# First FFN projections feature block by feature block over three weight tiles; the joins' lo parts and sums of squares on VectorE

## The chip, the cores and the metric

The kernel runs on one core of a Trainium2 chip. The metric is the device time of one execution in microseconds. All products run on TensorE (PE), which accumulates in PSUM banks. VectorE (DVE), ScalarE (ACT) and GpSimd (POOL) work between them, and SyncE (SP) issues the transfers. Each engine takes its instructions strictly in the order in which they stand in its own queue; semaphores make one wait for another.

## The reference

The reference is a two-layer backbone over 512 latent tokens and 256 context tokens of width 1024, in fp32:

```python
h = modulate(rmsnorm(x), m[0], m[1])
y = even_mixer(h_ctx, h_lat, ...) if i % 2 == 0 else odd_mixer(h_ctx, h_lat, ...)
x = x + m[2] * y
x = x + m[5] * conv_ffn(modulate(rmsnorm(x), m[3], m[4]), ffn_w_up[i], ffn_conv_w[i], ffn_conv_b[i], ffn_w_down[i])

def conv_ffn(h, w_up, conv_w, conv_b, w_down):
    u = h @ w_up                                  # 1024 -> 2 x 2816
    u = conv(u, width 3 over tokens) + conv_b
    a, gate = split(u, 2)
    return (a * silu(gate)) @ w_down
```

The even mixer (layer 0) is differential attention beside pooling, the odd one (layer 1) a gated linear recurrence in both directions. Both end in an output projection. In layer 1 the context is not carried on after the mixer. At the end stands `rmsnorm(x) * final_norm`.

## The kernel before

The streams lie with features on the partitions: eight feature blocks of 128 (`KT`), f = 0 to 7, tokens along the free axis. `xl` holds the latents, `xc` the context. An fp32 product is made of three matmuls with rounded parts: a value is split into a hi part, its rounding (ACT, L153 or L541), and a lo part, the rest (DVE, L154 or L542). `up` (L167) then adds, for each feature block, wh x hh, wh x hl and wl x hh into one PSUM bank; every matmul goes through the helper at L137. A weight tile is 128 x 1024 values: its wh comes from L153, its wl from L154.

A **join** is the stretch in which one stage's output projection ends and the next stage's first projection begins. There are four: A (even out-projection into FFN 0), B (last down-projection of FFN 0 into the odd mixer), C (odd out-projection into FFN 1) and D (last down-projection of FFN 1 into the final norm). At a join tokens go by 256: A and B have three such segments, two of latents and the context, C and D two. For each segment and each f, the following happens:

- PE makes the product into a bank, and `residual` (L198, DVE) adds it into the stream. Its read frees the bank.
- `acc_add` (L493 to L506) squares the new stream on ACT (L502 for f below 2, L505 for the others) and adds the square into one of two sums, `acc`, by L506. For f = 3, 4, 5 the sum runs on GpSimd, for 2, 6, 7 on DVE. The squares lie in two buffers.
- When all f are done, `norm` (L525) multiplies the sums by a matrix of ones on PE and takes rstd on ACT (L350, L352). Then, for each f, it scales (L540, DVE), makes hh (L541, ACT) and hl (L542, DVE).

The norm of a segment runs between the next segment's products. The last segment's is left over as an iterator, `self.todo`, which the next stage takes up: at A the norm of the context, at C that of the second half of the latents.

The FFN goes over 22 pairs of weight tiles. Its first pair is special. `ffn_pre` (L545) makes three of its four weight tiles ahead of time, during the out-projection; in layer 1 the lo parts of the second and third are made on GpSimd. `first_gated` (L609) then multiplies: for each segment, each block of 256 tokens and each of the three tiles, all eight f, so 24 matmuls in a row on one bank. The rest of `todo` is taken up after the third tile of the first block in layer 0, after the first tile in layer 1. The fourth tile is split after that (its buffers are those of the first tile) and multiplied over all tokens. `conv` and `gate` (L646, L654) follow on ACT and DVE. The banks of the FFN turn over seven PSUM tiles.

The Tile framework orders each engine's instructions from the program text and its own rules; the fences in the section on the change show what came of it.

Of the kernel before, what the change touches and what calls it, by code (L numbers as in the profile page):

```python
# [16 lines left out]
ALU = mybir.AluOpType  # L17
# [3 lines left out]
P = 128  # L21
D = 1024
KT = D // P
NL = 512
NC = 256
# [90 lines left out]
class Net:  # L116
# [376 lines left out]
    def acc_add(self, f, seg):  # L493
        nc = self.nc
        o, n = seg
        i = f % 2
        if f == 0:
            self.acc[o] = self.t(self.np, [P, 2, NC], "acc")
        acc = self.acc[o][:, i, :]
        x = self.xres(f, seg)  # L500
        if f < 2:
            nc.scalar.activation(acc, x, AF.Square)  # L502
            return
        sq = self.t(self.np, [P, NC], "sq2")
        nc.scalar.activation(sq, x, AF.Square)  # L505
        (nc.gpsimd if f in (3, 4, 5) else nc.vector).tensor_tensor(acc, acc, sq, op=ALU.add)  # L506

    def segmented(self, segs, body, then, first=3, rate=1, defer=False):
        todo = iter(())
# [35 lines left out]
    def ffn_pre(self, l):  # L545
        nc, Wu = self.nc, self.a["ffn_w_up"][l]
        ra, rg = self.load_cols(Wu, 0), self.load_cols(Wu, DFF)
        ws = []
        self.pre = (ra, rg, ws)
        for raw, j in ((ra, 0), (rg, 0), (ra, 1)):  # L550
            eng = nc.gpsimd if l and ws else nc.vector
            ws.append(self.split(raw[:, :, j * P:(j + 1) * P], eng=eng))
            yield

    def odd_pre(self):
# [53 lines left out]
    def first_gated(self, l, segs):  # L609
        nt = segs[-1][0] + segs[-1][1]  # L610
        ra, rg, ws = self.pre
        ws = list(zip((0, FT, 1), ws))
        cs = {i: self.t(self.tmp, [P, nt], "cv", bufs=4) for i, _ in ws}
        for seg in segs:
            o, n = seg
            outs = [self.t(self.ps, [P, NL], "mm", bufs=self.mmbufs)[:, :n] for _ in ws]
            for p in range(0, n, NC):
                for (i, w), out in zip(ws, outs):
                    self.up(w, out[:, p:p + NC], (o + p, NC))
                    if l or i == 1:  # L620
                        for _ in self.todo:
                            pass
            for (i, _), out in zip(ws, outs):
                self.conv(l, i, cs[i], out, seg)
        gs = [self.gate(cs[0], cs[FT])]
        i, w = FT + 1, self.split(rg[:, :, P:2 * P])
        cs[i] = self.t(self.tmp, [P, nt], "cv", bufs=4)
        for seg in segs:
            out = self.t(self.ps, [P, NL], "mm", bufs=self.mmbufs)[:, :seg[1]]
            self.up(w, out, seg)  # L630
            self.conv(l, i, cs[i], out, seg)
        return gs + [self.gate(cs[1], cs[i])]
# [779 lines left out]
```

## Time and profile before

| | us |
|---|---|
| median of three runs | 1778.73 |
| the runs | 1779.82, 1777.18, 1778.73 |
| profiled execution | 1778.03 |
| its span | 1776.2 |
| PE busy | 1730.6 (97%) |
| DVE busy | 1146.7 (65%) |
| ACT busy | 711.5 (40%) |
| POOL busy | 75.5 (4%) |

The mean granted clock of TensorE is 0.992 of full speed (2.4 GHz); at 0.50 it runs at 1.2 GHz. In a timeline row the first number is the start in us from the span's start, the second the duration, and what stands in brackets is the idle time of that engine just ahead, with the releaser that the profile infers. A duration contains a latency, so on a full engine the starts lie closer than the durations say.

### The profile page before, as it was taken

To read this page: it belongs to the slowest core of one execution; us is meant where nothing else is said; L and a number is where in the kernel's file an instruction comes from. 1 tells how busy PE (TensorE), PEld (TensorE's weight loads), DVE (VectorE), ACT (ScalarE), POOL (GpSimd) and SP (SyncE) were. 2 spreads that over 40 slices of the span, in tenths; PEclk is the share of its full clock that TensorE was granted. 3 is DMA by queue.
4 is the path that set the end of the run, shared out by engine and by line. 5 is a ranking of instruction groups with operands and counts; after the bars stand their busy time and mean duration, and the time that the engine had idled before them with its cause. 6 is when DMAs were issued, how large, how long until landed. Compare 5 with 4: busy or idle time off the path is not lost.

```text
span 1776.2 us, 29058 instructions
## 1 busy us (share of the span) xinstructions
PE 1730.6 (97%) x12223; PEld 1471.9 (83%) x12223; DVE 1146.7 (65%) x2109; ACT 711.5 (40%) x1310; POOL 75.5 (4%) x80
## 2 busy tenths in 40 slices
PE   7899989999999999999999999999999999999998
PEld 4687878888888888888889888888878888888887
DVE  5534786785556555656568356666798866656657
ACT  4435564453223232222345424444454533333334
POOL 0202210010000000000001000000000200000001
PEclk9999989999999999999999999999999999999999
DMA  9233113334323432323130211111212132232231
GB/s 319 87 98 97 47 46 104 113 119 167 119 96 116 146 119 96 119 95 119 48 119 1 89 58 49 49 49 49 73 49 95 49 99 91 95 113 86 87 118 48
DMA packets 115478, 165.78 MB, mean 93 GB/s; under 512 B 3211, under 2 KB 98579, under 8 KB 115347
## 3 DMA queue, kind: packets, MB, share of 16 engines
q1 hardware_dynamic: 115043, 163.76, 27.4%
q8 instruction: 96, 1.57, 0.4%
q14 instruction: 35, 0.29, 0.0%
q10 hardware_dynamic: 304, 0.16, 0.0%
HBM read 161.82 MB, written 2.10 MB: 92 GB/s over the span
## 4 chain that ended last, share of the span: by engine, by line
PE 90%; DVE 5%; ACT 2%; DMA 1%; issue 1%; POOL 0%; SPq 0%; DVEq 0%; ACTq 0%; POOLq 0%
PE mm L137 78%; PE sc L137 3%; PE o L137 2%; PE pm L137 2%; PE lv L137 2%; PE tr L137 1%; DVE sq L540 1%; PE tp L1328 1%; DVE hl L542 1%; DMA mraw<-in_w_mod_dram 1%; PE tr L1032 0%; DMA raw<-in_ev_w_in_dram 0%; DVE xl L198 0%; DVE wl L154 0%; ACT wh L153 0%
## 5 line engine op out<-in xcount | busy, mean ns | idle before, releaser
L137 PE MATMUL mm<-hh,wh 128*128 128x512 f32 (+1 forms) x1800 | 636.3, 354 | 5.6 <-ACT hh L541 3.9
L137 PE MATMUL mm<-hh,wl 128*128 128x512 f32 (+1 forms) x1800 | 625.2, 348 | 0.0
L137 PE MATMUL mm<-hl,wh 128*128 128x512 f32 (+1 forms) x1800 | 623.9, 347 | 0.0
L137 PEld LDWEIGHTS mm<-hh,wh 128*128 128x128 f32 x1800 | 339.1, 189 | 57.1 <-issue 10.7
L137 PEld LDWEIGHTS mm<-hh,wl 128*128 128x128 f32 x1800 | 339.2, 188 | 44.4
L137 PEld LDWEIGHTS mm<-hl,wh 128*128 128x128 f32 x1800 | 339.4, 189 | 42.5
L154 DVE TENSOR_TENSOR wl<-raw,wh 128x1024 fp32r<-128x1024 f32 x193 | 234.7, 1225 | 215.3 <-ACT wh L153 211.7
L153 ACT ACTIVATE wh<-raw 128x1024 fp32r<-128x1024 f32 x195 | 203.9, 1057 | 387.7 <-PE mm L137 369.9
L650 DVE SCALAR_TENSOR_TENSOR cv<-mm,colC,cv 128x511 f32<-128x511 f32 (+1 forms) x264 | 173.3, 658 | 112.5 <-ACT cv L648 108.9
L198 DVE SCALAR_TENSOR_TENSOR xl<-mm,mod,xl 128x512 f32<-128x512 f32 (+1 forms) x252 | 170.8, 687 | 45.1 <-PE mm L137 44.8
L137 PE MATMUL mm<-gh,wh 128*128 128x512 f32 (+1 forms) x448 | 159.6, 356 | 0.0
L137 PE MATMUL mm<-gh,wl 128*128 128x512 f32 (+1 forms) x448 | 159.5, 356 | 0.0
L137 PE MATMUL mm<-gl,wh 128*128 128x512 f32 (+1 forms) x448 | 159.3, 356 | 0.0
L648 ACT ACTIVATE cv<-mm,colC 128x512 f32<-128x512 f32 (+1 forms) x132 | 91.6, 695 | 144.2 <-PE mm L137 144.2
L137 PEld LDWEIGHTS mm<-gh,wl 128*128 128x128 f32 x448 | 84.1, 188 | 13.1
L137 PEld LDWEIGHTS mm<-gl,wh 128*128 128x128 f32 x448 | 84.1, 188 | 13.0
L137 PEld LDWEIGHTS mm<-gh,wh 128*128 128x128 f32 x448 | 84.1, 188 | 12.8
L137 PE MATMUL mm<-wh,hh 128*128 128x256 f32 x288 | 82.3, 286 | 2.0 <-DVE xc L198 1.2
L137 PE MATMUL mm<-wl,hh 128*128 128x256 f32 x288 | 80.4, 279 | 0.0
L137 PE MATMUL mm<-wh,hl 128*128 128x256 f32 x288 | 80.3, 279 | 0.0
L655 ACT ACTIVATE cv<-cv 128x768 f32<-128x768 f32 (+1 forms) x44 | 32.5, 739 | 92.0 <-DVE cv L650 92.0
L506 POOL TENSOR_TENSOR acc<-acc,sq 128x256 f32<-128x256 f32 x30 | 23.5, 786 | 1047.2 <-ACT sq L505 1046.8
(271 smaller groups left out, 2195.2 us busy)
## 6 DMA issues: line engine op xcount, KB each, us to landing
raw<-in_ffn_w_up_dram SPq DMA_DIRECT2D x44, 1024.0 KB, 5.1
mraw<-in_w_mod_dram SPq DMA_DIRECT2D x14, 2048.0 KB, 7.9
raw<-in_ffn_w_down_dram SPq DMA_DIRECT2D x22, 1024.0 KB, 4.8
raw<-in_hg_w_in_dram SPq DMA_DIRECT2D x20, 1024.0 KB, 5.0
raw<-in_w_mod_dram SPq DMA_DIRECT2D x12, 1024.0 KB
raw<-in_ev_w_in_dram SPq DMA_DIRECT2D x8, 1024.0 KB, 5.3
mraw<-in_w_mod_dram SPq DMA_DIRECT2D x16, 512.0 KB, 10.0
raw<-in_ev_w_out_dram SPq DMA_DIRECT2D x4, 1024.0 KB, 4.9
```

The lines of the kernel that those rows point to most:

```text
L137: self.nc.tensor.matmul(out, lhsT=lhsT, rhs=rhs, start=start, stop=stop)
L153: insts = (self.nc.scalar.activation(hi, view, AF.Copy), (eng or self.nc.vector).tensor_tensor(lo, view, hi.bitcast(F32), op=ALU.subtract))
L154: (eng or self.nc.vector).tensor_tensor(lo, view, hi.bitcast(F32), op=ALU.subtract))
L198: self.nc.vector.scalar_tensor_tensor(x, in0=out, scalar=gate[:, f, cond:cond + 1], in1=x, op0=ALU.mult, op1=ALU.add)
L506: (nc.gpsimd if f in (3, 4, 5) else nc.vector).tensor_tensor(acc, acc, sq, op=ALU.add)
L540: nc.vector.scalar_tensor_tensor(xn, in0=x, scalar=sc, in1=r, op0=ALU.mult, op1=ALU.mult)
L542: nc.vector.scalar_tensor_tensor(hl, in0=xn, scalar=sh, in1=hh.bitcast(F32), op0=ALU.add, op1=ALU.subtract)
L648: self.nc.scalar.activation(c[:, o:o + n], out, AF.Identity, scale=self.conv_col(l, 1, i), bias=self.conv_col(l, 3, i))
L650: self.nc.vector.scalar_tensor_tensor(c[:, o + d:o + n - s], in0=out[:, s:n - d], scalar=self.conv_col(l, tap, i), in1=c[:, o + d:o + n - ...
L655: self.last_silu = self.nc.scalar.activation(cg, cg, AF.Silu)
L1328: self.nc.tensor.transpose(tp[:, c:c + P], in_=p[:, half * 384 + c:half * 384 + c + P], identity=self.ident)
```

## The change

Three edits. First, L506 runs on DVE for every f: 30 sums move from GpSimd, nine at A, nine at B, six at C and six at D. Second, in layer 1 `ffn_pre` makes the lo parts of the second and third tile on DVE. Third, `first_gated` goes over f in the outer loop and over the three tiles in the inner: nine matmuls for each f, three on each bank. The rest of `todo` is taken up after f = 2, that is after 27 matmuls.

```diff
         sq = self.t(self.np, [P, NC], "sq2")
         nc.scalar.activation(sq, x, AF.Square)
-        (nc.gpsimd if f in (3, 4, 5) else nc.vector).tensor_tensor(acc, acc, sq, op=ALU.add)
+        nc.vector.tensor_tensor(acc, acc, sq, op=ALU.add)
...
         for raw, j in ((ra, 0), (rg, 0), (ra, 1)):
-            eng = nc.gpsimd if l and ws else nc.vector
-            ws.append(self.split(raw[:, :, j * P:(j + 1) * P], eng=eng))
+            ws.append(self.split(raw[:, :, j * P:(j + 1) * P]))
             yield
...
             for p in range(0, n, NC):
-                for (i, w), out in zip(ws, outs):
-                    self.up(w, out[:, p:p + NC], (o + p, NC))
-                    if l or i == 1:
+                for f in range(KT):
+                    for (i, w), out in zip(ws, outs):
+                        self.up(w, out[:, p:p + NC], (o + p, NC), (f,))
+                    if f == 2:
                         for _ in self.todo:
                             pass
```

What this makes of PE's queue at join A. `mm_669`, `mm_670` and `mm_671` are the banks of the first, second and third weight tile; the first `mm_671` waits for the residual that empties the last bank of the out-projection, `mm_659`. Before, `mm_669` has 24 matmuls and then `mm_670` 24; this is where `mm_671` begins:

```order
L137 MATMUL mm_670_3815<-hh_8_91,wl_603_3481 128x256
L137 MATMUL mm_670_3815<-hh_8_91,wh_602_3480 128x256
L137 MATMUL mm_670_3815<-hl_9_92,wh_602_3480 128x256
L137 MATMUL mm_670_3815<-hh_8_91,wl_603_3481 128x256
L137 MATMUL mm_671_3816<-hh_8_91,wh_610_3517 128x256
L137 MATMUL mm_671_3816<-hl_9_92,wh_610_3517 128x256
```

Now, from the end of the out-projection on:

```order
L137 MATMUL mm_659_3767<-hh_8_91,q_594_3450 128x256
L137 MATMUL mm_669_3814<-hh_8_91,wh_597_3457 128x256
L137 MATMUL mm_669_3814<-hl_9_92,wh_597_3457 128x256
L137 MATMUL mm_669_3814<-hh_8_91,wl_598_3458 128x256
L137 MATMUL mm_670_3815<-hh_8_91,wh_602_3480 128x256
L137 MATMUL mm_670_3815<-hl_9_92,wh_602_3480 128x256
L137 MATMUL mm_670_3815<-hh_8_91,wl_603_3481 128x256
L137 MATMUL mm_671_3816<-hh_8_91,wh_610_3517 128x256
```

The third tile's first matmul was the 49th of the FFN and is now the seventh.

DVE's queue at join C, up to the last residual, that of `mm_1894`, for which the first matmul of FFN 1 waits. `wl_1874` is the third tile's lo part, `acc` the sum of squares. Before:

```order
L540 SCALAR_TENSOR_TENSOR sq_1887_13704<-xl_6_89,mod14_1079_7385,acc_1855_13554 128x256
L198 SCALAR_TENSOR_TENSOR xl_6_89<-mm_1888_13708,mod12_926_6101,xl_6_89 128x256
L540 SCALAR_TENSOR_TENSOR sq_1890_13719<-xl_6_89,mod14_1079_7385,acc_1855_13554 128x256
L542 SCALAR_TENSOR_TENSOR hl_9_92<-sq_1887_13704,mod13_1014_6814,hh_8_91 128x256
L198 SCALAR_TENSOR_TENSOR xl_6_89<-mm_1891_13723,mod12_926_6101,xl_6_89 128x256
L540 SCALAR_TENSOR_TENSOR sq_1893_13734<-xl_6_89,mod14_1079_7385,acc_1855_13554 128x256
L198 SCALAR_TENSOR_TENSOR xl_6_89<-mm_1894_13738,mod12_926_6101,xl_6_89 128x256
```

And now:

```order
L506 TENSOR_TENSOR acc_1878_13655<-acc_1878_13655,sq2_1889_13716 128x256
L540 SCALAR_TENSOR_TENSOR sq_1890_13719<-xl_6_89,mod14_1079_7385,acc_1855_13554 128x256
L198 SCALAR_TENSOR_TENSOR xl_6_89<-mm_1891_13723,mod12_926_6101,xl_6_89 128x256
L154 TENSOR_TENSOR wl_1874_13633<-raw_1856_13556,wh_1873_13632 128x1024
L542 SCALAR_TENSOR_TENSOR hl_9_92<-sq_1890_13719,mod13_1014_6814,hh_8_91 128x256
L506 TENSOR_TENSOR acc_1878_13655<-acc_1878_13655,sq2_1892_13731 128x256
L540 SCALAR_TENSOR_TENSOR sq_1893_13734<-xl_6_89,mod14_1079_7385,acc_1855_13554 128x256
L198 SCALAR_TENSOR_TENSOR xl_6_89<-mm_1894_13738,mod12_926_6101,xl_6_89 128x256
```

Sums that GpSimd made, and the third tile's lo part, stand ahead of the last residual. From the residual of `mm_1860` on (the first of three in the row at 1382.08 below) up to that of `mm_1894`, the queue held 14 residuals, 4 sums, 3 of L540 and 1 of L542; now it holds 14, 11 sums, 2 lo parts of weights, 3 and 2. The same count at A, from the residual at 353.65 to that of `mm_659`, differs by nine sums alone.

PE's queue at join C, where the fourth tile (`wh_1918`) begins. Its split waits until the first tile, `wh_1858`, is no longer read. Before, the last matmul that reads `wh_1858` stands 38 places ahead of this:

```order
L137 MATMUL mm_1906_13783<-hh_8_91,wh_1873_13632 128x256
L137 MATMUL mm_1906_13783<-hl_9_92,wh_1873_13632 128x256
L137 MATMUL mm_1906_13783<-hh_8_91,wl_1874_13633 128x256
L137 MATMUL mm_1921_13985<-hh_8_91,wh_1918_13980 128x512
L137 MATMUL mm_1921_13985<-hl_9_92,wh_1918_13980 128x512
L137 MATMUL mm_1921_13985<-hh_8_91,wl_1919_13981 128x512
```

And now:

```order
L137 MATMUL mm_1904_13781<-hl_9_92,wh_1858_13560 128x256
L137 MATMUL mm_1904_13781<-hh_8_91,wl_1859_13561 128x256
L137 MATMUL mm_1905_13782<-hh_8_91,wh_1865_13595 128x256
L137 MATMUL mm_1905_13782<-hl_9_92,wh_1865_13595 128x256
L137 MATMUL mm_1905_13782<-hh_8_91,wl_1866_13596 128x256
L137 MATMUL mm_1906_13783<-hh_8_91,wh_1873_13632 128x256
L137 MATMUL mm_1906_13783<-hl_9_92,wh_1873_13632 128x256
L137 MATMUL mm_1906_13783<-hh_8_91,wl_1874_13633 128x256
L137 MATMUL mm_1921_13985<-hh_8_91,wh_1918_13980 128x512
L137 MATMUL mm_1921_13985<-hl_9_92,wh_1918_13980 128x512
L137 MATMUL mm_1921_13985<-hh_8_91,wl_1919_13981 128x512
```

The last reader of the first tile's hi part moved to eight places ahead of the fourth tile's first matmul. At A sixteen matmuls of another task (`pm`, modulation of the next layer) stand between the two as well. GpSimd's queue shrinks from 80 to 48 rows, SP's order stays.

## Rows read from the trace of the kernel before

**Rows 1.** Page, part 1: busy time and share of each engine.

```profile
PE 1730.6 (97%) x12223; PEld 1471.9 (83%) x12223; DVE 1146.7 (65%) x2109; ACT 711.5 (40%) x1310; POOL 75.5 (4%) x80
```

**Rows 2.** Timeline of PE at join A: first and 49th matmul of FFN 0.

```profile
372.98 0.28 PE L137 MATMUL mm<-hh,wh 128*128 128x256 f32 x1
...
378.63 0.28 PE L137 MATMUL mm<-hh,wh 128*128 128x256 f32 x1
```

**Rows 3.** Timeline of DVE at join A.

```profile
355.16 1.76 DVE L154 TENSOR_TENSOR wl<-raw,wh 128x1024 fp32r<-128x1024 f32 x1
...
375.05 0.96 DVE L542 SCALAR_TENSOR_TENSOR hl<-sq,mod,hh 128x256 fp32r<-128x256 f32 x1
...
376.33 0.47 DVE L542 SCALAR_TENSOR_TENSOR hl<-sq,mod,hh 128x256 fp32r<-128x256 f32 x1
376.72 0.47 DVE L540 SCALAR_TENSOR_TENSOR sq<-xl,mod,acc 128x256 f32<-128x256 f32 x1
377.12 0.41 DVE L506 TENSOR_TENSOR acc<-acc,sq 128x256 f32<-128x256 f32 x1
377.45 0.47 DVE L198 SCALAR_TENSOR_TENSOR xc<-mm,mod,xc 128x256 f32<-128x256 f32 x1
```

**Rows 4.** Windows at A and C: length, busy of each engine, PEclk, DMA, GB/s.

```profile
353.65:377.45 23.80, 21.44 (x165) 20.00 (x165) 23.36 (x52) 14.61 (x37) 7.38 (x9) 1.00 0.29 93
1382.08:1395.94 13.86, 10.40 (x81) 9.69 (x79) 11.87 (x24) 8.25 (x19) 9.25 (x8) 0.99 0.00 1
```

**Rows 5.** Timeline of PE at join C.

```profile
1392.38 0.28 PE L137 MATMUL mm<-hh,q 128*128 128x256 f32 x1
1396.56 0.55 PE L137 MATMUL mm<-hh,wh 128*128 128x256 f32 x1 [3.90 <-ACT hh L541]
1396.91 0.42 PE L137 MATMUL mm<-hl,wh 128*128 128x256 f32 x1
1397.12 0.41 PE L137 MATMUL mm<-hh,wl 128*128 128x256 f32 x1
```

**Rows 6.** Timeline of DVE at join C.

```profile
1380.95 1.22 DVE L154 TENSOR_TENSOR wl<-raw,wh 128x1024 fp32r<-128x1024 f32 x1
1382.08 1.26 DVE L198 SCALAR_TENSOR_TENSOR xl<-mm,mod,xl 128x256 f32<-128x256 f32 x3
...
1384.03 0.68 DVE L506 TENSOR_TENSOR acc<-acc,sq 128x256 f32<-128x256 f32 x1
...
1393.81 2.21 DVE L540 SCALAR_TENSOR_TENSOR sq<-xl,mod,acc 128x256 f32<-128x256 f32 x1
1395.94 0.47 DVE L198 SCALAR_TENSOR_TENSOR xl<-mm,mod,xl 128x256 f32<-128x256 f32 x1
```

**Rows 7.** Timeline of POOL at join C: the third tile's lo part.

```profile
1393.39 2.35 POOL L154 TENSOR_TENSOR wl<-raw,wh 128x1024 fp32r<-128x1024 f32 x1 [0.18 <-ACT wh L153]
```

**Rows 8.** Timeline of PE: two other gaps, early in the program.

```profile
60.13 1.13 PE L137 MATMUL mm<-k,c 128*128 128x512 f32 x2 [1.58 <-ACT k L448]
...
224.23 0.33 PE L1369 MATMUL tp<-ident,sq 128*128 128x128 f32 x1 [2.28 <-ACT sq L1363]
```

**Rows 9.** Windows after gaps of 1.58, 2.28 and 3.90 us.

```profile
60.20:64.00 3.80, 2.28 (x6) 0.92 (x7) 3.10 (x7) 2.65 (x5) 1.82 (x2) 1.00 0.62 169
224.50:228.20 3.70, 3.70 (x18) 3.36 (x17) 2.73 (x10) 1.82 (x5) 0.00 (x0) 0.55 0.01 2
1396.56:1402.45 5.89, 5.89 (x23) 5.53 (x24) 4.31 (x12) 2.95 (x7) 0.00 (x0) 0.50 0.55 178
```

**Rows 10.** Timeline of ACT and DVE: split of the fourth weight tile at C.

```profile
1413.02 1.06 ACT L153 ACTIVATE wh<-raw 128x1024 fp32r<-128x1024 f32 x1 [1.83 <-PE mm L137]
...
1414.11 1.23 DVE L154 TENSOR_TENSOR wl<-raw,wh 128x1024 fp32r<-128x1024 f32 x1 [2.40 <-ACT wh L153]
```

**Rows 11.** Timeline of DVE at join B: first and last of five stretched rows.

```profile
948.41 0.85 DVE L540 SCALAR_TENSOR_TENSOR sq<-xl,mod,acc 128x256 f32<-128x256 f32 x1
...
961.18 0.96 DVE L542 SCALAR_TENSOR_TENSOR hl<-sq,mod,hh 128x256 fp32r<-128x256 f32 x1
```

## The prediction

> **What bounds the kernel now.** I read the page's first part first: TensorE (PE) is busy for 97% of the span [rows 1]. A microsecond that PE loses is a microsecond of the whole, unless it already stood idle there; what another engine gains or loses counts only where PE waits for it. So I went to the four places where the moved work lies, the joins: A (even out-projection into FFN 0, 353 to 391 us), B (FFN 0 into the odd mixer, 938 to 965), C (odd out-projection into FFN 1, 1381 to 1397) and D (the end, from 1753).
>
> At A the reader is to see two things. PE runs the FFN's first block of 72 matmuls, begun at 372.98, without a break, 0.118 us apart: the 49th starts at 378.63 [rows 2]. Beside it VectorE (DVE) is full: 23.36 of 23.80 us between 353.65 and 377.45, so 0.44 us idle [rows 4]. DVE's residual L198 at 377.45 is the last of the out-projection [rows 3]; it frees a bank, and the 49th matmul, first of the third weight tile, needs that bank. It comes at 377.92, 0.7 us early, and nobody notices.
>
> At C, PE starts its last out-projection matmul at 1392.38 and FFN 1's first only at 1396.56, after 3.90 us idle [rows 5]. The profile's row names ACT's hh, but that was long done; the program's wait is for the last residual, 1395.94 + 0.47 = 1396.41 [rows 6]. That one stood behind an L540 of 2.21 us, beside which GpSimd made the third tile's lo part for 2.35 us [rows 7]. PE then runs at 1.2 GHz (granted clock 0.50 for 5.89 us, to 1402.45) [rows 9], matmuls 0.21 apart [rows 5].
>
> **DVE beside GpSimd.** L540 and L542 take 0.47 us, L506 0.41, a 1024-wide lo part L154 1.22; their starts on a full DVE lie 0.40, 0.39, 0.33 and 1.13 apart, and three L198 in 1.26 us are 0.395 apart [rows 3, 6]. Where GpSimd works, such rows stretch, L198 (which reads PSUM) does not. Taking each stretched row's excess over these durations: at A eight rows from 355.16 (1.76 for 1.22) to 375.05 (0.96 for 0.47) [rows 3], 2.65 us together; at C four from 1384.03 (0.68) to 1393.81 (2.21) [rows 6], 2.86; at B five from 948.41 (0.85) to 961.18 (0.96) [rows 11], 2.40.
>
> **The change, join A.** Nine sums more on DVE, all ahead of the last residual: 9 x 0.33 = 2.97. The stretch goes: -2.65. The residual starts at 377.45 + 2.97 - 2.65 = 377.77, less at most the 0.44 of idle that the sums can fill: 377.33 to 377.77. I take 377.6, and 378.1 for its end. So far a cost of near nothing, as the 49th matmul was due at 378.63. But the block's new order makes the third tile's first matmul the seventh instead of the 49th. The old one's seventh place was 372.98 + 6 x 0.118 = 373.69. PE cannot pass it (it works in order), so everything from there on, which ran without a break before, runs from 378.1: **+4.4 us** (4.15 to 4.6). The wait that the trace shows will be shorter, about 3.8, since the bank of the first FFN matmul also comes free some 0.5 later.
>
> Then the clock. A gap of 1.58 us left it alone; after 2.28 us [rows 8] the granted clock was 0.55 for 3.70 us, after 3.90 it was 0.50 for 5.89 [rows 9]. Each half-clock microsecond costs 1 - 0.118/0.212 = 0.44: 1.6 and 2.6. The new gap is nearest to the 3.90: **+2.6**; bounds 0 (no fall) and 2.6. What A does afterwards (normalization of the context, three convolutions at once) I cost at nothing: DVE then has 0.80 of work per feature (L540, L542) against 9 x 0.118 = 1.06 on PE. If that cover fails, it is the last rival below.
>
> **Join C.** Between the residuals of 1382.08 and the last, DVE's order now holds 14 L198, 2 lo parts, 11 sums and 5 L540/L542: 14 x 0.395 + 2 x 1.13 + 11 x 0.33 + 5 x 0.395 = 13.40 us, so 1395.48 at the earliest. From the other side: 1395.94, plus two lo parts 2.26, seven more sums ahead 2.31, one more L542 0.40, less the stretch 2.86, is 1398.05; and up to 1.99 us of the old idle [rows 4] can be filled, which gives 1396.06. I take 1396.1, ending 1396.57 against 1396.41: +0.15 (-0.45 to +2.1). So the gap of about 3.9 us and the half clock stay. Taking the features in turn gives nothing here: PE had no further wait for a feature after 1396.56.
>
> One wait is new. The fourth weight tile's split needs the buffers of the first tile. Before, the first tile's last hl matmul stood 38 places ahead of the fourth tile's first, 38 x 0.118 = 4.5 us; the split ran at 1413.02 and its lo part from 1414.11 for 1.23 [rows 10], and PE lost nothing. Now it stands eight places ahead. From that matmul's start t: it ends at t + 0.28 (the latency of the row at 1392.38), L153 takes 1.06 [rows 10] to t + 1.34, PE would be there at t + 8 x 0.118 = 0.94: 0.4 lost. L154 ends 1.23 [rows 10] after that, t + 2.57, and PE needs it two 512-wide matmuls later, four times the 0.118 or 0.46 after its restart at 1.34, so at 1.80: 0.8 lost. **+1.2** (0.9 to 1.3). At A sixteen other matmuls stand in that place, 1.9 us, and hide it. C together: **+1.35**.
>
> **Joins B and D.** At B three of nine moved sums fall where DVE still waits for PE, six into the full stretch: 6 x 0.33 - 2.40 = **-0.4**, between -2.4 (sums cost nothing) and +2.0 (the stretch stays). At D six sums go to a DVE that waits for PE between residuals: **0**, between -0.4 and +2.0, the six on the path. POOL's queue and SP's lose or keep their rows, nobody waits there.
>
> **Sum.** 4.4 + 2.6 + 1.35 - 0.4 = **+8.0 us**. On the profiled execution, 1778.03, that is 1786.0; the median of the three runs shown is 0.70 higher, so I say 1786.7.
>
> **Rivals.** *The clock holds at A.* The gap is cut by short work on both sides and A shows no fall: +5.4, 1784.1. For it: the 1.58 gap; against it: 2.28 and 3.90, with 3.8 at the far end.
>
> *GpSimd's whole time stood in DVE's way* (the side of faster). If all of GpSimd's busy time, 7.38 us at A and 9.25 at C [rows 4], had held DVE back and not only the stretch that I counted, then at A the residual ends by 373.5 and the seventh matmul never waits; at C it is only bounded by the last out-projection matmul, the gap falls to some 0.6, and the half clock with it: -3.3 - 2.6 + 1.2 = -4.7, 1774.0. It decides from a relief of about 6.8 us at A (377.45 + 2.97 + 0.47 - 6.8 = 374.1, when PE gets there) and 2.3 at C (a gap of 1.6). Against it: durations on DVE without GpSimd are known from the same stretch, and 0.44 us of idle is all that is left unexplained at A. The Trainium skill, "SBUF — State Buffer", section "Who interferes with whom", says that a DVE instruction with two SBUF inputs and a GpSimd instruction that reads SBUF shut each other out for a whole instruction. By that rule the relief could be up to GpSimd's whole time, the 1774.0 above; the rows agree in kind (L540 stretches, L198 with one PSUM input does not), not in that size.
>
> *The clock no longer falls at C*, because gap and work there lie otherwise, nor at A: 4.4 + 1.35 - 2.6 - 0.4 = +2.75, 1781.5, within what a measurement can tell from no change (0.2%, 3.6 us).
>
> *DVE becomes the bound of the first blocks.* If ACT and DVE deliver a feature not in 0.80 but in 1.36 us, eight features at A and eight at C are late by 0.3 each: +4.8 more, 1791.5. It needs hh, hl and the sums to alternate badly; the 0.26 us of slack per feature speaks against it.
>
> **How the numbers follow.** Forecast 0.60, clock holds at A 0.16, faster 0.09, no measurable change 0.08, DVE-bound 0.07. The first, second and last are slower by over 0.2%: 0.83. The range reaches from the third rival, less part of B's gain, to the last one: 1780.5 to 1791.
>
> **What would show it.** Right: after the sixth FFN 0 matmul a PE gap of 3 to 4 us near 374, released by L198, then a clock of 0.5; DVE rows of 0.47 without stretch; the gap at C still 3 to 4 us; two short PE waits before and after the fourth tile's first two matmuls at C. Wrong: a seventh matmul that runs on, or a gap at C below 2 us.

## The result, and the profile after

The changed kernel takes **1788.57 us** in the median (1784.26 to 1791.11), the kernel before on the same chip 1778.73 (1777.18 to 1782.09): ratio **1.0054, 95% interval 1.0034 to 1.0074**, that is 9.6 us more (6.0 to 13.2). The profiled execution has a span of 1786.8, 10.6 more than before's.

Page, part 1, after: busy time and share of each engine, as [rows 1].

```profile
PE 1737.6 (97%) x12223; PEld 1477.2 (83%) x12223; DVE 1148.9 (64%) x2141; ACT 712.3 (40%) x1310; POOL 46.2 (3%) x48
```

The work is the same, PE only needs 7 us more for it: PE at half clock counts as busy, at A and also ahead of the change (below). DVE took over 32 instructions from POOL and is busy for just 2.2 us more.

**Join A.** Timeline of PE after (start, duration, instruction, idle time ahead and its releaser), as [rows 2]. The first row is FFN 0's first matmul, the third its sixth, the fourth its seventh.

```profile
375.90 0.28 PE L137 MATMUL mm<-hh,wh 128*128 128x256 f32 x1
...
376.47 0.28 PE L137 MATMUL mm<-hh,wl 128*128 128x256 f32 x1
380.41 0.58 PE L137 MATMUL mm<-hh,wh 128*128 128x256 f32 x1 [3.67 <-DVE xc L198]
380.79 0.41 PE L137 MATMUL mm<-hl,wh 128*128 128x256 f32 x1
```

After six matmuls PE stands for 3.67 us, and the releaser is L198, the residual; the matmuls behind are 0.21 apart instead of 0.12. Timeline of DVE after, as [rows 3]:

```profile
354.55 1.22 DVE L154 TENSOR_TENSOR wl<-raw,wh 128x1024 fp32r<-128x1024 f32 x1
...
379.15 0.48 DVE L540 SCALAR_TENSOR_TENSOR sq<-xl,mod,acc 128x256 f32<-128x256 f32 x1
379.54 0.42 DVE L506 TENSOR_TENSOR acc<-acc,sq 128x256 f32<-128x256 f32 x1
379.88 0.48 DVE L198 SCALAR_TENSOR_TENSOR xc<-mm,mod,xc 128x256 f32<-128x256 f32 x1
```

The 1.76 us lo part of [rows 3] is 1.22 now, and no L540 or L542 is stretched. The last row is the residual for which PE waits: it ends at 380.36, PE starts 0.05 later.

Windows after, as [rows 4] and [rows 9] (length, busy time of PE, PEld, DVE, ACT, POOL, PEclk, DMA, GB/s): two at A, two at C.

```profile
380.41:384.00 3.59, 3.59 (x17) 3.59 (x18) 3.52 (x9) 2.20 (x5) 0.00 (x0) 0.53 0.62 256
384.00:386.00 2.00, 2.00 (x16) 1.90 (x15) 1.47 (x4) 1.20 (x3) 0.00 (x0) 1.00 0.03 8
1406.43:1412.20 5.77, 5.77 (x32) 5.67 (x33) 4.73 (x12) 2.62 (x7) 0.00 (x0) 0.70 0.50 170
1412.20:1416.00 3.80, 3.80 (x35) 3.80 (x34) 2.56 (x6) 2.18 (x5) 0.00 (x0) 1.00 0.00 0
```

The granted clock fell to half at A, for 3.4 us (0.53 is the mean of the first 3.59 us). At C it is at half for a shorter part than in [rows 9]: by the 0.70, for 3.4 of the 5.77 us.

**Join C.** Timeline of PE after, as [rows 5]: first matmul of FFN 1, then the last before the fourth tile and the fourth tile's first, third and fifth.

```profile
1406.43 0.36 PE L137 MATMUL mm<-hh,wh 128*128 128x256 f32 x1 [3.85 <-ACT hh L541]
...
1425.75 0.28 PE L137 MATMUL mm<-hh,wl 128*128 128x256 f32 x1
1426.35 0.50 PE L137 MATMUL mm<-hh,wh 128*128 128x512 f32 x1 [0.33 <-ACT wh L153]
...
1427.61 0.50 PE L137 MATMUL mm<-hh,wl 128*128 128x512 f32 x1 [0.52 <-DVE wl L154]
...
1428.19 0.39 PE L137 MATMUL mm<-hl,wh 128*128 128x512 f32 x1
```

The gap at C is as long as before (3.85 for 3.90). The two waits around the fourth tile are new, 0.33 and 0.52. What they cost is read from the starts, since the idle time in brackets begins only at the modelled end of the matmul ahead: from 1425.75 to 1428.19 are 2.44 us, and without waits they would be one step of 0.12 and four of 0.23, that is 1.04. So **1.4**. Timeline of DVE after, as [rows 6] and, for the first row, as the last of [rows 11] at B:

```profile
961.22 0.48 DVE L542 SCALAR_TENSOR_TENSOR hl<-sq,mod,hh 128x256 fp32r<-128x256 f32 x1
...
1403.54 1.22 DVE L154 TENSOR_TENSOR wl<-raw,wh 128x1024 fp32r<-128x1024 f32 x1
...
1405.40 0.49 DVE L540 SCALAR_TENSOR_TENSOR sq<-xl,mod,acc 128x256 f32<-128x256 f32 x1
1405.80 0.49 DVE L198 SCALAR_TENSOR_TENSOR xl<-mm,mod,xl 128x256 f32<-128x256 f32 x1
```

L540 has lost its 2.21 us, but the third tile's lo part, 1.22, stands in DVE's queue instead, with the sums.

**Where the time went.** I cut each timeline at the same rows of ACT: the first split of the out-projection's weights (`ud<-raw`, L153), the third gate of FFN 0 (`gh<-cv`), its last, the first `k` of the odd mixer, the first split of the odd out-projection's weights (`V<-raw`), the third gate of FFN 1, its last, and the end. "Start" is all ahead of the first cut, where none of the kernels differ. Each figure is the length of the stage less that in the kernel before, in us; each is one execution. The spans are read to 0.1 us, so D and the span are good to 0.1.

| kernel | start | A | FFN 0 | B, odd mixer | C | D | span |
|---|---|---|---|---|---|---|---|
| after | +2.02 | +6.64 | +1.21 | -0.59 | +0.81 | +0.51 | +10.60 |
| loop_only | -1.19 | +6.03 | 0 | +0.02 | +0.35 | +0.07 | +5.30 |
| moves_only | +3.25 | +0.87 | 0 | -0.82 | +0.46 | +0.72 | +4.50 |
| hold_third | -2.50 | +5.51 | +0.02 | -0.70 | +0.75 | +0.54 | +3.60 |
| fill_gap | +3.70 | +4.75 | 0 | -0.53 | +0.55 | +0.50 | +9.00 |
| hold_drain | -2.99 | +0.95 | +0.01 | -0.71 | +0.82 | +0.52 | -1.40 |
| freed | +2.44 | +0.53 | +0.10 | -0.84 | -1.66 | +0.53 | +1.10 |
| freed_lag | -2.81 | +0.66 | +1.20 | +0.24 | +0.40 | +0.51 | +0.20 |
| freed_moves | -2.39 | +0.43 | +0.01 | -0.80 | +1.99 | +0.63 | -0.10 |
| freed_tail | +3.69 | +0.67 | +1.20 | -0.65 | -1.19 | +0.48 | +4.20 |
| tail_gpsimd | -2.25 | +0.08 | +0.11 | -0.69 | +0.27 | +0.08 | -2.40 |

(FFN 1 between its third and last gate differs by 0.03 at most and is left out.) The start varies by 7 us in code that is the same in all of them, so it is not of the change; it is why one profile cannot decide a matter of 3 us here and a stage can. It goes with the granted clock there. Windows over the start, of hold_drain (-2.99) and of fill_gap (+3.70):

```profile
10.00:300.00 290.00, 270.91 (x1828) 222.03 (x1827) 177.90 (x421) 146.15 (x332) 40.05 (x34) 0.98 0.35 113
10.00:300.00 290.00, 270.84 (x1784) 219.22 (x1782) 171.25 (x408) 141.82 (x322) 39.99 (x34) 0.95 0.32 105
```

The same window has 0.98 in all five kernels whose start is 2.2 to 3.0 shorter, 0.97 in before and loop_only, 0.96 in freed and after, and 0.95 in the three whose start is 3.2 to 3.7 longer. The +1.2 in FFN 0 comes in three of eleven traces, with the same PE instructions as in the others and no change of the clock. It belongs to no edit that I can name (freed has +0.10, freed_tail +1.20, and they differ only at the end of C). By PE's starts 1.1 of it lies between the 256-wide matmuls, which come 0.1045 apart in the mean instead of 0.1038; why, I have not found. What is left of after's difference, A, B, C and D, is 6.64 - 0.59 + 0.81 + 0.51 = **7.4 us**, inside the interval of the ratio.

### The profile page after: what moved, and what is told of

It is laid out like the page before. It is cut to its first block, busy times and chain, and to the rows that moved or that the text cites. A ratio compares the mean times of both kernels' runs of the same rounds, so it can differ in the third digit from the quotient of the medians.

```text
span 1786.8 us, 29034 instructions
## 1 busy us (share of the span) xinstructions
PE 1737.6 (97%) x12223; PEld 1477.2 (83%) x12223; DVE 1148.9 (64%) x2141; ACT 712.3 (40%) x1310; POOL 46.2 (3%) x48
## 4 chain that ended last, share of the span: by engine, by line
PE 91%; DVE 5%; ACT 1%; DMA 1%; issue 1%; SPq 0%; DVEq 0%; ACTq 0%
PE mm L137 79%; PE sc L137 3%; PE o L137 3%; PE pm L137 2%; PE lv L137 2%; PE tr L137 1%; PE tp L1328 1%; DVE wl L154 1%; DMA mraw<-in_w_mod_dram 1%; DVE acc L506 1%; PE tr L1032 0%; DVE sq L540 0%; DVE xl L198 0%; DVE hl L542 0%; DVE xc L198 0%
## 5 line engine op out<-in xcount | busy, mean ns | idle before, releaser
L153 ACT ACTIVATE wh<-raw 128x1024 fp32r<-128x1024 f32 x195 | 204.1, 1058 | 395.7 <-PE mm L137 375.1
L198 DVE SCALAR_TENSOR_TENSOR xl<-mm,mod,xl 128x512 f32<-128x512 f32 (+1 forms) x252 | 170.8, 689 | 42.0 <-PE mm L137 41.3
L198 DVE SCALAR_TENSOR_TENSOR xc<-mm,mod,xc 128x256 f32<-128x256 f32 x104 | 50.2, 484 | 18.5 <-PE mm L137 18.5
```

The costliest lines, as they stand in the source:

```text
L153: insts = (self.nc.scalar.activation(hi, view, AF.Copy), (eng or self.nc.vector).tensor_tensor(lo, view, hi.bitcast(F32), op=ALU.subtract))
L198: self.nc.vector.scalar_tensor_tensor(x, in0=out, scalar=gate[:, f, cond:cond + 1], in1=x, op0=ALU.mult, op1=ALU.add)
```

## The experiments

Kernels with the same figure for before were timed together, and each ratio is to the runs of before taken with it.

| kernel | median us (range) | before us | ratio, 95% interval |
|---|---|---|---|
| loop_only | 1783.5 (1782.36 to 1785.62) | 1776.26 | 1.0043, 1.0030 to 1.0056 |
| moves_only | 1778.42 (1775.39 to 1783.5) | 1776.26 | 1.0008, 0.9996 to 1.0021 |
| hold_third | 1782.69 (1776.37 to 1788.86) | 1776.26 | 1.0035, 1.0018 to 1.0051 |
| fill_gap | 1783.07 (1780.1 to 1787.0) | 1776.26 | 1.0037, 1.0023 to 1.0051 |
| hold_drain | 1779.45 (1775.12 to 1784.79) | 1777.35 | 1.0014, 1.0001 to 1.0028 |
| freed | 1778.65 (1774.59 to 1781.82) | 1777.35 | 1.0005, 0.9992 to 1.0017 |
| freed_lag | 1776.24 (1772.52 to 1781.68) | 1777.35 | 0.9996, 0.9984 to 1.0008 |
| freed_moves | 1778.64 (1775.53 to 1784.23) | 1777.35 | 1.0014, 1.0001 to 1.0026 |
| freed_tail | 1775.76 (1771.44 to 1782.62) | 1776.01 | 0.9996, 0.9983 to 1.0009 |
| tail_gpsimd | 1777.4 (1771.83 to 1783.83) | 1776.01 | 1.0005, 0.9991 to 1.0018 |

Diffs are against the changed kernel unless said otherwise.

**Theory:** edit 3, by moving the third tile's first matmul ahead of the residual that frees its bank, costs a wait and a half clock at A; edits 1 and 2 are worth next to nothing. **Rivals:** the sums on DVE are what costs; or the order by features costs something of its own (DVE and ACT too slow for it).

### Edit 3 alone, and edits 1 and 2 alone

loop_only keeps the new loop and puts sums and lo parts back:

```diff
-        nc.vector.tensor_tensor(acc, acc, sq, op=ALU.add)
+        (nc.gpsimd if f in (3, 4, 5) else nc.vector).tensor_tensor(acc, acc, sq, op=ALU.add)
...
-            ws.append(self.split(raw[:, :, j * P:(j + 1) * P]))
+            eng = nc.gpsimd if l and ws else nc.vector
+            ws.append(self.split(raw[:, :, j * P:(j + 1) * P], eng=eng))
```

> Only the loop order of first_gated is changed; the sums and lo parts stay on GpSimd as in the kernel before. Theory (the third tile's bank): the seventh FFN matmul at A waits for the last residual, 3.5 to 4 us, with a half clock behind it, and the fourth tile waits about 0.9 at C: 6 to 8 us slower than before, most of the change's 9.8. Rival (DVE's added load is what costs): within 1.5 us of before.

Timeline of PE in loop_only (seventh matmul at A), then a window behind it, then its DVE:

```profile
376.69 0.38 PE L137 MATMUL mm<-hh,wh 128*128 128x256 f32 x1 [4.14 <-DVE xc L198]
```

```profile
376.60:380.00 3.40, 3.31 (x18) 3.31 (x19) 3.33 (x10) 1.94 (x4) 0.00 (x0) 0.61 0.48 195
```

```profile
353.91 1.76 DVE L154 TENSOR_TENSOR wl<-raw,wh 128x1024 fp32r<-128x1024 f32 x1
```

moves_only keeps sums and lo parts on DVE and goes tile by tile again:

```diff
-                for f in range(KT):
-                    for (i, w), out in zip(ws, outs):
-                        self.up(w, out[:, p:p + NC], (o + p, NC), (f,))
-                    if f == 2:
+                for (i, w), out in zip(ws, outs):
+                    self.up(w, out[:, p:p + NC], (o + p, NC))
+                    if l or i == 1:
```

> Only the sums and lo parts are moved to DVE; the loop order is that of before, so the third tile's first matmul is the 49th again. Theory (bank): the residual that ends near 378 is in time for it, the gap at C stays near 3.9: within 1.5 us of before. Rival (DVE's load): 6 to 9 us slower. Rival (GpSimd's interference was the price): 4 to 5 us faster.

Window of moves_only over the first FFN matmuls at A:

```profile
377.20:385.20 8.00, 8.00 (x70) 8.00 (x69) 7.93 (x21) 4.89 (x11) 0.00 (x0) 1.00 0.71 264
```

In loop_only the whole wait at A is there (4.14 us), with sums on GpSimd and DVE's rows stretched as before. A is 6.03 longer, of after's 6.64, and the whole run 7.6 us (5.3 to 9.9), as expected. In moves_only no FFN matmul waits at A, and A is 0.87 longer. So the loss is edit 3's. What the two edits to DVE do by themselves is 0.87 at A, -0.82 at B and the odd mixer, +0.46 at C, +0.72 at D: 1.2 in all, in an interval (-0.7 to +3.7 us) that holds zero. The rival that the sums cost the time is out, and so is the one that they bring much: 4 to 5 us faster lies outside that interval.

### The third tile later at A

hold_third takes, in FFN 0's first block alone, the first two tiles feature by feature and the third as a whole behind them:

```diff
             for p in range(0, n, NC):
+                if l == 0 and o + p == 0:
+                    for f in range(KT):
+                        for (i, w), out in zip(ws[:2], outs):
+                            self.up(w, out[:, p:p + NC], (o + p, NC), (f,))
+                        if f == 2:
+                            for _ in self.todo:
+                                pass
+                    self.up(ws[2][1], outs[2][:, p:p + NC], (o + p, NC))
+                    continue
```

> The changed kernel, but in the first block of FFN 0 only two tiles go feature by feature, and the third follows with its 24 matmuls. Theory (bank): no gap of 3.7 us at A and no half clock there; what is left is the fourth tile's wait at C, 0.9, and up to 1 us of DVE's load at A: 0.5 to 2.5 us slower than before. Rival (the loop order itself, through waits for features or weight loads): 6 us slower or more.

Timeline of PE in hold_third, its only idle row behind the first FFN matmul at A, then of DVE: the last two sums of the context and, between them, the last residual.

```profile
375.91 2.35 PE L137 MATMUL mm<-acc,ones 128*128 128x256 f32 x4 [2.23 <-DVE xc L198]
```

```profile
375.05 0.41 DVE L506 TENSOR_TENSOR acc<-acc,sq 128x256 f32<-128x256 f32 x1
375.38 0.47 DVE L198 SCALAR_TENSOR_TENSOR xc<-mm,mod,xc 128x256 f32<-128x256 f32 x1
...
376.56 0.41 DVE L506 TENSOR_TENSOR acc<-acc,sq 128x256 f32<-128x256 f32 x1
```

The expectation missed. PE still waits, but now at the norm's product with the ones (four matmuls into one `mm` tile), which the order by features has moved ahead to the 19th place, and the granted clock is 0.51 from 375.91 to 379.30. Two things hold the product there. One is a bank: it starts 0.06 after the last residual ends (375.38 + 0.47 = 375.85), whose result its first half does not use, so it seems to have been given the bank of the last residual. The other is its own data: the two sums that it multiplies end at 375.46 and 376.97. The sums alone would have held its first half until 375.46 and its second until 376.97; at most 0.4 us of the 2.23 is the bank's. The norm, too, is taken up too early here.

hold_drain therefore takes the norm up behind the third tile as well, which removes both reasons:

```diff
             for p in range(0, n, NC):
+                if l == 0 and o + p == 0:
+                    for f in range(KT):
+                        for (i, w), out in zip(ws[:2], outs):
+                            self.up(w, out[:, p:p + NC], (o + p, NC), (f,))
+                    self.up(ws[2][1], outs[2][:, p:p + NC], (o + p, NC))
+                    for _ in self.todo:
+                        pass
+                    continue
```

> As hold_third, but the context's norm is taken up behind the third tile, at the place that it had in the kernel before; in hold_third its ones product took the bank of the last residual at the 19th place and waited 2.2 us for it, and as long for the sums. Theory (the wait belongs to the bank, whoever takes it): at A no PE gap over 1 us in the first FFN block, A within 1 us of the kernel with the moves alone; in all 1 to 3 us slower than before (its moves 1.4, the fourth tile at C 0.9). Rival (the order feature by feature costs by itself): 5 us slower or more.

Windows of hold_drain over the first FFN matmuls at A:

```profile
372.00:376.00 4.00, 4.00 (x38) 4.00 (x37) 4.00 (x11) 2.37 (x6) 0.00 (x0) 1.00 0.96 368
376.00:380.00 4.00, 4.00 (x34) 3.89 (x33) 3.88 (x10) 2.42 (x5) 0.00 (x0) 1.00 0.37 147
```

PE is busy throughout at full clock, and A is 0.95 longer than before: 5.7 us of the 6.64 are back, and what is left is moves_only's 0.87. All other blocks still go feature by feature, so that order costs nothing by itself at A; DVE and ACT keep up.

### The price of the half clock

fill_gap puts 30 matmuls, whose results are overwritten, ahead of FFN 0's first, so that PE is busy while it waits. They add work and change no result.

```diff
             outs = [self.t(self.ps, [P, NL], "mm", bufs=self.mmbufs)[:, :n] for _ in ws]
+            if l == 0 and o == 0:
+                for g in range(30):
+                    self.mm(outs[0][:, 0:NC], ws[0][1][0][:, 0, :], self.hh[:, 0, 0:NC], True, True)
```

> The changed kernel with 30 more matmuls ahead of the first FFN matmul at A, products into the first tile's bank that its first real matmul overwrites: 3.5 us of work in place of the wait. Theory: the wait of the seventh matmul falls below 1 us, its start stays where it was, and the clock does not fall there: 1.5 to 2.6 us faster than the changed kernel, 7 to 8.5 slower than before. Rival (the half clock costs nothing, since PE would wait for features anyway): like the changed kernel, 9 to 10.5 slower than before.

Timeline of PE in fill_gap (the 30 with the first FFN matmul, then the seventh), and windows:

```profile
377.55 3.81 PE L137 MATMUL mm<-hh,wh 128*128 128x256 f32 x31
...
382.03 0.38 PE L137 MATMUL mm<-hh,wh 128*128 128x256 f32 x1
```

```profile
376.00:382.00 6.00, 5.94 (x48) 5.74 (x48) 6.00 (x17) 4.12 (x11) 0.00 (x0) 1.00 0.59 205
382.00:386.00 4.00, 3.97 (x30) 3.86 (x31) 3.89 (x10) 2.46 (x5) 0.00 (x0) 1.00 0.55 221
```

The gap is filled, the clock stays at 1.00, and A is 4.75 longer instead of 6.64. The seventh matmul starts where it did (382.03 - 3.70 = 378.33; after 380.41 - 2.02 = 378.39), so the 1.9 us between the two is the half clock's price and the late bank has the rest. That is read from one execution of each; the ratios, 1.0037 and 1.0054, have intervals that overlap. In this stage thirty matmuls for nothing save time.

### The last product in another bank

freed lets the last product of the last segment, at A and at C, go into a bank of its own tag (`o`) that no FFN tile takes. The reason of the wait goes, and not only its place. A second thing changes with it: the norm is taken up after f = 5. Its product then starts at 382.45, behind the end of its last sum (381.89), and does not wait; after f = 2 it would have stood near 375.98 + 27 x 0.118 = 379.2, an estimate, and waited for that sum. The bank without this was not run. The seventh matmul stands ahead of both places, so what becomes of its wait is the bank's doing.

```diff
-                    if f == 2:
+                    if f == 5:
...
-            out = self.t(self.ps, [P, NL], "mm", bufs=3)[:, :seg[1]]
+            last = then and f == KT - 1 and seg == HALF[-1]
+            out = self.t(self.ps, [P, NL], "o" if last else "mm", bufs=1 if last else 3)[:, :seg[1]]
...
-            out = self.out_bank(f + 1, (seg[0], seg[1], 0), True)
+            out = self.t(self.ps, [P, NL], "o", bufs=1)[:, :seg[1]] if f == KT - 1 and seg == segs[-1] else self.out_bank(f + 1, (seg[0], seg[1], 0), True)
```

> The changed kernel, but the last output projection of A and of C is accumulated in a bank that no weight tile of the FFN takes, and the last norm is taken up after f = 5 instead of f = 2. Theory (bank): the 3.7 us at A go, and the 3.85 at C too, in whose place PE waits for the third weight tile and for features, some 1 to 3 us in pieces; no half clock at A: 7 to 13 us faster than the changed kernel, 3 us faster to 2 slower than before. Rival (DVE is too late with everything at C, so the wait only changes its name): C stays, 4 to 7 us faster than the changed kernel.

Timeline of PE in freed (the first FFN matmul at A; at C the ninth, which reads the third tile's lo part, and a later one), then windows at C: up to the gap, and three behind it.

```profile
375.98 0.39 PE L137 MATMUL mm<-hh,wh 128*128 128x256 f32 x1 [0.20 <-DVE xc L198]
...
1397.89 0.39 PE L137 MATMUL mm<-hh,wl 128*128 128x256 f32 x1 [1.05 <-DVE wl L154]
...
1400.21 0.38 PE L137 MATMUL mm<-hl,wh 128*128 128x256 f32 x1 [0.26 <-DVE hl L542]
```

```profile
1393.50:1396.84 3.34, 3.34 (x27) 3.01 (x25) 3.26 (x9) 3.00 (x7) 0.00 (x0) 1.00 0.00 0
1397.89:1400.10 2.21, 1.99 (x11) 1.49 (x11) 2.21 (x7) 1.10 (x3) 0.00 (x0) 1.00 0.45 125
1400.10:1403.50 3.40, 3.29 (x27) 3.29 (x28) 3.22 (x9) 1.44 (x4) 0.00 (x0) 1.00 0.67 234
```

At A the wait is gone. At C the gap of 3.85 has shrunk to 1.05, which the third tile's lo part sets, and the clock holds: C is 1.66 shorter than before, 2.5 shorter than in after. So the wait at C was that of a bank as well. With two banks chosen otherwise and the norm later, the changed kernel cannot be told from the kernel before (ratio 1.0005 for 1.0054, some 9 us).

freed_moves is freed with the loop tile by tile, as before (the loop's diff is that of moves_only); freed_lag is freed with the third tile three features behind in every block, and the norm after f = 6:

```diff
-                for f in range(KT):
-                    for (i, w), out in zip(ws, outs):
-                        self.up(w, out[:, p:p + NC], (o + p, NC), (f,))
-                    if f == 2:
+                for f in range(KT + 3):
+                    for j, ((i, w), out) in enumerate(zip(ws, outs)):
+                        g = f - 3 * (j == 2)
+                        if 0 <= g < KT:
+                            self.up(w, out[:, p:p + NC], (o + p, NC), (g,))
+                    if f == 6:
```

> As freed, with the loop order of the kernel before (tile by tile). It asks what the new order is worth once the bank is free. Theory: tile by tile needs a new feature every 0.36 us, DVE has one in some 0.9, so at C PE waits about 4 us in pieces where the order by features (1.06 us of work each) waits less: 1 to 3 us slower than freed_lag, about like before or up to 2 faster. Rival (the order is worth nothing): equal to freed within 0.5.

> As freed, with the third tile three features behind the other two in every block. Theory: PE no longer meets the third tile's split at C, which at the earliest is over 2.3 us behind the last out-projection matmul, and the first tile is free nine matmuls earlier for the fourth tile's split, so its 0.85 us go: 1 to 3 us faster than freed, 1 to 5 faster than before. Rival (features alone set the pace at C): within 1 us of freed.

Windows of freed_moves at C:

```profile
1391.00:1396.00 5.00, 2.14 (x8) 1.15 (x7) 4.97 (x12) 2.42 (x6) 0.00 (x0) 1.00 0.39 131
1396.00:1402.00 6.00, 5.77 (x20) 4.88 (x21) 3.70 (x10) 2.71 (x6) 0.00 (x0) 0.51 0.19 67
```

Timeline of PE in freed_lag at C, all its idle rows behind the out-projection, and windows:

```profile
1393.68 0.39 PE L137 MATMUL mm<-hh,wh 128*128 128x256 f32 x1 [0.41 <-ACT hh L541]
...
1395.06 0.39 PE L137 MATMUL mm<-hl,wh 128*128 128x256 f32 x1 [0.99 <-DVE hl L542]
...
1396.33 0.58 PE L137 MATMUL mm<-hh,wh 128*128 128x256 f32 x1 [0.33 <-ACT hh L541]
```

```profile
1392.00:1395.70 3.70, 2.29 (x16) 1.82 (x14) 3.70 (x9) 1.92 (x4) 0.00 (x0) 1.00 0.01 1
1395.70:1396.30 0.60, 0.29 (x2) 0.01 (x1) 0.60 (x3) 0.54 (x2) 0.00 (x0) 0.50 0.88 154
1396.00:1402.00 6.00, 5.61 (x24) 5.32 (x25) 5.00 (x13) 2.88 (x7) 0.00 (x0) 0.50 0.53 172
```

Tile by tile with the bank free, PE runs straight into the features that are not ready, and C is 1.99 longer than before; by features, freed, it is 1.66 shorter. So in these executions the new loop pays at C once the bank is out of the way. Of the 3.65 between them some 2.6 is the half clock (0.51 over 6 us, at 0.44 each), which freed did not have, and the ratios, 1.0014 and 1.0005, have intervals that overlap. freed_moves was expected about like before and came 2.5 us slower (0.2 to 4.6).

freed_lag removes the waits around the fourth tile, and pays with the clock: it is at half for 6 us from 1395.70 on. By then there had been two gaps, of 0.41 and 0.99 us; the third, 0.33, ends later. That does not fit the prediction's picture of one long gap. The expected gain over freed, 1 to 3 us, is not shown: C is 2.06 longer, and the ratios overlap.

### A better tail, and the same code at two clocks

freed_tail is freed with the third tile three features behind only in the very last block at C, so that nine matmuls lie between the first tile's last reader and the fourth tile. tail_gpsimd is freed_tail with edits 1 and 2 undone (the diff of loop_only).

```diff
-                for f in range(KT):
-                    for (i, w), out in zip(ws, outs):
-                        self.up(w, out[:, p:p + NC], (o + p, NC), (f,))
+                lag = 3 if l and o + p + NC == nt else 0
+                for f in range(KT + lag):
+                    for j, ((i, w), out) in enumerate(zip(ws, outs)):
+                        g = f - lag * (j == 2)
+                        if 0 <= g < KT:
+                            self.up(w, out[:, p:p + NC], (o + p, NC), (g,))
                     if f == 5:
```

> The run freed, and in the very last block of 256 tokens of FFN 1's first three tiles (join C) the third tile goes three features behind the other two, so that 9 of its matmuls stand between the last reader of the first tile and the fourth tile. Nothing changes ahead of that block. Theory (the fourth tile's wait is a matter of places alone, and the clock at C held in freed because its gap there was 1.05 us with full work around it): no gap at A, at C the one gap of about 1 us at the third tile's lo part and granted clock 1.00 to the end of C, fourth tile's first matmul without a wait and 0 to 0.2 us at its third. C about 2.4 us shorter than in the kernel before (freed 1.66), the whole about 2 us below the kernel before apart from the spread of the start, ratio 0.997 to 1.000. Rival (the clock at C is a matter of chance from execution to execution once there is any gap): granted clock 0.50 for some 6 us after the gap, and C at about +0.2 instead.

> The kernel before with edit 3 (feature by feature) and the two freed banks and the tail of the last block, but with the sums of f = 3, 4, 5 and the two lo parts on GpSimd as before: edits 1 and 2 undone in freed_tail. Theory (edits 1 and 2 give about 0.8 us at B and odd mixer, cost 0.5 at A and 0.5 at D, and at C the third tile's lo part is ready at about the same time on either engine, 1395.75 on the clock of before on GpSimd against 1395.5 on DVE): within 1 us of freed_tail; A near 0, B near 0, D near 0; at C a gap of 1 to 2.1 us at the ninth matmul, that of the third tile's lo part, now released by GpSimd, DVE rows stretched beside it. Rival (at C the lo part on GpSimd comes late, and the gap of 2 us or more brings the half clock back): granted clock 0.50 for about 6 us, C 2.6 us longer than in freed_tail.

Timeline of PE in freed_tail at C, all idle rows behind the out-projection, and the windows that answer to those of freed:

```profile
1400.40 0.39 PE L137 MATMUL mm<-hh,wl 128*128 128x256 f32 x1 [1.04 <-DVE wl L154]
...
1402.71 0.58 PE L137 MATMUL mm<-hl,wh 128*128 128x256 f32 x1 [0.26 <-DVE hl L542]
```

```profile
1396.00:1399.34 3.34, 3.34 (x27) 3.04 (x25) 3.24 (x9) 3.01 (x7) 0.00 (x0) 1.00 0.00 0
1400.40:1402.60 2.20, 1.99 (x11) 1.49 (x11) 2.20 (x7) 1.09 (x3) 0.00 (x0) 1.00 0.39 126
1402.60:1406.00 3.40, 3.29 (x15) 3.29 (x16) 3.21 (x9) 1.43 (x4) 0.00 (x0) 0.50 0.68 234
```

The waits at the fourth tile are gone, as the theory has it (no idle row there; by the starts 0.3 us at its third matmul is left). The clock, though, went the rival's way, for 3.4 us and not 6: up to there the two programs are the same, the first two windows agree to 0.01 us in length and in PE's busy time, and yet freed runs on at 1.00 with 27 matmuls in the last window and freed_tail at 0.50 with 15. The twelve missing matmuls are 12 x 0.118 = 1.4 us; with them C would be 2.6 shorter than before, near the 2.4 expected. So the program up to there does not settle whether the clock falls behind such a gap.

Timeline of PE in tail_gpsimd at C (an earlier wait, then the matmul that waits for the lo part) and a window behind it:

```profile
1391.04 0.39 PE L137 MATMUL mm<-hl,wh 128*128 128x256 f32 x1 [0.77 <-DVE hl L542]
...
1393.30 0.58 PE L137 MATMUL mm<-hh,wl 128*128 128x256 f32 x1 [1.16 <-POOL wl L154]
```

```profile
1393.30:1400.00 6.70, 6.43 (x28) 6.13 (x29) 5.83 (x15) 3.22 (x7) 0.00 (x0) 0.50 0.49 160
```

The lo part on GpSimd leaves nearly the same gap, 1.16 for 1.04, but ahead of it stands one of 0.77 that freed_tail does not have, and here the clock is at half for all of the 6.7 us. A and D are as before (+0.08 each), which leaves 0.6 and 0.4 to the sums on DVE there. B and the odd mixer were expected near 0 and are 0.69 shorter, as they are with the sums on DVE (-0.65); so that gain is not shown to be the sums'. Edits 1 and 2 move nothing that the runs can tell: 0.9996 and 1.0005 with intervals that overlap. No kernel here beats the one before by more than its interval.

## Why the prediction was right

**The sum:** 8.0 predicted, 7.4 found in the four stages, 9.6 (6.0 to 13.2) in the runs. The stages came at 6.6 for 7.0 (A), 0.8 for 1.35 (C), -0.6 for -0.4 (B with the odd mixer) and 0.5 for 0 (D), so the errors partly cancel.

- **The wait at A, +4.4.** Right in mechanism and size. The old seventh place is 373.69, or 375.71 with after's start 2.02 later; the matmul came at 380.41, so +4.7. Of the 0.3 that I missed nearly all is the last residual: predicted to end at 378.1, it ended at 380.36 - 2.02 = 378.34. The first FFN matmul came 0.9 later, not 0.5, and so the visible wait is 3.67 (predicted 3.8); that splits the loss and does not change it. loop_only shows edit 3 as the cause. The bank as its means is shown by the row itself (the matmul waits for a residual that it does not read) and by freed, where the same matmul runs on; hold_drain fits it.
- **The half clock at A, +2.6.** Right in kind, over-sized: the clock fell for 3.4 us, not 5.9, and cost 1.9 by fill_gap. I had carried the length of C's fall [rows 9] over to A; [rows 8] with 3.70 us after a gap of 2.28 gave 1.6, and lay as near.
- **The gap at C, +0.15, and its half clock, unchanged.** The residual came 0.58 late instead of 0.15 (1405.80, less the 9.28 by which after is behind at the cut ahead of C, against 1395.94), inside the bounds. The half clock was shorter than before; what is left of C's +0.81 after this 0.58 and the fourth tile's 1.4 is -1.2. Most of it is the clock: before it stood at half for 5.89 us, after for 3.4, and 2.5 us less are 1.1 by the prediction's rate. The prediction's unchanged half clock there was a guess, since by freed and freed_tail the clock can go either way. That the 3.9 us hang on a bank, freed bears out: there PE runs on behind the out-projection.
- **The fourth tile, +1.2.** The two waits came where they were predicted. By the starts they cost 1.4: 0.48 ahead of the first matmul (1426.35 for 1425.87; predicted 0.4), 0.80 ahead of the third (0.8), and 0.1 as PE starts again. freed_tail took them away by places alone.
- **B, -0.4:** -0.43 at B itself, but that is not shown to be the prediction's reason. tail_gpsimd has -0.41 there with the sums on GpSimd and DVE's rows still stretched, loop_only -0.11. The number may be luck. **D, 0:** +0.51 in after and +0.07 in loop_only, so six sums do lie partly on the path at the end. I had put them beside waits for PE; of their 6 x 0.33 = 2.0 us a quarter did not fit there.
- **The rivals.** That GpSimd's whole time stood in DVE's way is out: with the sums off GpSimd the residual started 0.41 later (379.88 - 2.02 against 377.45), near the +2.97 - 2.65 = +0.32 of my terms; with a relief of 6.8 it would have come 3.8 earlier. The Trainium skill, "SBUF — State Buffer", "Who interferes with whom", says that a DVE instruction with two SBUF inputs contends with a GpSimd instruction that reads SBUF; the rows agree in kind (with GpSimd's sums gone the 1.76 us row is 1.22), but the relief was not the whole of GpSimd's time. That the clock holds at A is out by its 0.53. That DVE bounds the first blocks is out at A: from 384 to 386 PE is full at 1.00, and hold_drain's order by features has no idle row in the 8 us shown.
- **The measured 1788.57** is 1.9 above the forecast. The profiled execution, whose time is that median, has 2.0 in the start and 1.2 in FFN 0, neither of the change and neither in the sum.

Left open: what makes the 1.2 us in FFN 0, why the clock in the start differs from execution to execution, and what the free bank is worth with the norm left after f = 2.

## What to carry to other kernels

When a loop is turned so that more accumulators are opened early, look up for each new early user which bank it gets and whose last read frees that bank: PE works in order, so one bank that is late holds up the whole interleaved block, while the old order hid it behind 48 matmuls. The same holds for data: the norm's product, taken up early too, waited for its sums as soon as the third tile was out of its way. Choosing another bank for the one last product and taking the norm later gave back what the new order lost. And before work is moved off an engine, see whether what waits at the end was held by that engine or by the sum of the queue: here the moved work and the relief cancelled to half a microsecond.

## What the runs showed of the hardware

**The clock can fall without one long gap.** It fell behind gaps of 0.41 and 0.99 us close together (freed_lag, 0.50 for 6 us), while a single one of 1.58 had left it alone [rows 8, 9].

**The same instructions with the same gap ran at both clocks.** Behind 1.05 and 0.26 us of idle freed stayed at 1.00, behind 1.04 and 0.26 freed_tail went to 0.50 for 3.4 us. The Trainium skill, "TensorE: Matmul & The Clock Gate", Part 1, says that the gate judges activity in a window that runs free and does not start with the kernel; this pair fits that, though two executions do not prove it. So for a gap of about 1 us I would forecast a chance of a fall and not a yes or no. Its price in a single execution was 1.4 us in freed_tail and, by 0.44 for each of the 6.7 us, 2.9 in tail_gpsimd.

**Sums on GpSimd cost DVE about what it would take to make them.** At A nine of them, 2.97 us of work on DVE, moved the last residual by 0.41, because the stretched rows went with them. Over the whole program, thirty sums and two lo parts on GpSimd (tail_gpsimd, 1.0005) or on DVE (freed_tail, 0.9996) make no difference that the intervals can tell.
